# Half of v as seven block products, and the gate row's dot products in quarter pieces: one layer of a gated attention block on one core

## The chip, the cores and the metric

The kernel runs on 1 core of one Trainium2 chip. The metric is device time in microseconds (us) of one execution; lower is better. The core has five engines that work beside each other: TensorE (PE) multiplies matrices, VectorE (DVE) and ScalarE (ACT) work on elements, GpSimd (POOL) here mostly issues adding transfers, and SyncE (SP) issues the plain transfers. Each runs its own list of instructions in order; semaphores tie them together. PE writes its results to PSUM, eight banks of 128 x 512 floats. Everything else lies in SBUF, 128 partitions.

## The reference

One layer, batch 1, 512 tokens, width 2048, float32:

```
shift, scale, gate = silu(c) @ W_ada + b_ada                  # one row each
h = rmsnorm(x) * (1 + scale) + shift
[q_lat|kv_lat|k_rope|z_mla|u|v|z_sgu|g_mla|g_sgu] = h @ W_in
A = causal latent attention(q_lat, kv_lat, k_rope) * silu(z_mla)
B = u * (tril(W_s) @ rmsnorm(v) + b_s) * silu(z_sgu)          # per chunk of 128 tokens, 16 groups
x = x + gate * ((sigmoid(g_mla) * A + sigmoid(g_sgu) * B) @ W_out)
out = rmsnorm(x)
```

What matters here: `v` is 2048 columns of `h @ W_in`, 512 tokens by 2048 inputs. Its groups of 128 columns are needed one by one when B is computed, with a norm over all 2048 columns. The row `gate` is needed only at the very end.

## The kernel before

Each float32 operand of a large product is split in two float32r parts, a high one (a cast on ACT) and the rest (a subtraction on DVE), and each product is three matmuls: high x high, high x low, low x high (`mm3`). Weights come as granules of up to 1024 columns by 128 partitions (512 KB). `Stream` (line 60) loads them into three raw buffers and splits each into one of two pairs of part buffers: `get(i)` (line 110) sees to it that granule i+1 is being split while i is multiplied (`split_to`, line 91) and that loads are issued three ahead (`dma_to`, line 77). A split so waits for PE to finish with the granule two before it.

The work goes in stages, written out by hand:

1. The latent columns, while `scale` and `shift` are made as dot products on DVE: each of 16 rows of W_ada per vector is a transfer of 1 MB (`ada_load`, 306) and one DVE instruction over 2048 elements (`ada_dot`, 312).
2. The v stage (line 511 on): v and the rope key, in five groups of columns, 512, 512, 384, 384 and 320 wide (`VW`, line 38), eight granules each. The tokens' h is stationary, the weights move. A granule holds two of 16 chunks of the inputs; each goes against four blocks of tokens, three matmuls each: 24 matmuls. The groups alternate between two sets of four PSUM banks. After a group, `evac_v` (541) squares and copies one bank per step on ACT and stores it to `v_d` in DRAM. Beside the granules DVE and ACT do the `early` work: latents are scaled and stored (`lat_scale`), sums of h's quarters are made (`make_sums`, 475) and split for the next stage (two of them, s1 and s2, at once; s3 and s4 are kept and split later, s4 in steps 32 to 39, s3 in slots -2 and -1 of the next stage, line 806), and the 16 dot products of `gate` run in steps 8 to 30 (331 to 335), each on a tile of 1 MB loaded through SP's queue.
3. The gate stage: the five gates' 10240 columns as pairs of heads, seven block products per pair (a Strassen-Winograd form: products of sums of h and sums of weights in place of eight products). There it is the weights that are stationary. It has 266 slots, one product each, with an order written by a planner. `on(s, phase, f)` puts a piece of work into slot s; within a slot the lists go FIRST, EVAC, GATE, SPLIT, BACK, then the slot's matmuls, then MISC and LOAD. `place(s, us, f)` (590) seeks the first slot from s on whose DVE time, with the cost `us` given by hand, stays below 2.6 or 2.7 us. The split of a slot's weights is put two slots ahead; there are three pairs of part buffers. Sums of weights are made by transfers that add to what lies in the buffer, issued by POOL.
4. Attention, the output product, the final norm.

Branch B runs inside stage 3, a pair of groups at a time (lines 812 to 857). With S the slot in which the pair's spatial weights are masked: `v_load` (820) fetches each of the two pieces of v, 256 KB, at S-3 into the tiles lat10 (even group) and lat11 (odd); ACT scales the even one in slot S+1 (`sgu_scale`, 828), PE mixes it at the end of S+2 (`sgu_mix`, 833); the odd one is scaled in S+3 and mixed at the end of S+4; DVE adds the bias. There are eight pairs. Such a tile name is one buffer: a new tile of that name waits until the last reader of the old one is done.

Of the kernel before, what the change touches and what calls it, by code (L numbers as in the profile page):

```python
# [37 lines left out]
VW = (512, 512, 384, 384, 320)  # L38
# [21 lines left out]
class Stream:  # L60
# [12 lines left out]
    def add(self, ap, n, to=None):  # L73
        self.src.append((ap, n, to))
        return len(self.src) - 1

    def dma_to(self, i):
        i = min(i, len(self.src) - 1 if self.limit is None else self.limit)
        while self.n_dma <= i:
            k = self.n_dma  # L80
            for f in self.before.pop(k, ()):
                f()
            ap, n, _ = self.src[k]
            pool, tag = self.raws[self.next_raw]
            self.next_raw = (self.next_raw + 1) % len(self.raws)
            t = pool.tile([P, GW], F32, tag=tag, name=f"{tag}_{k}")
            self.nc.sync.dma_start(t[:, :n], ap)
            self.raw[k] = t
            self.n_dma += 1

    def split_to(self, i):
        i = min(i, len(self.src) - 1)
        while self.n_split <= i:
            k = self.n_split
            self.dma_to(k)
            _, n, to = self.src[k]
            raw = self.raw.pop(k)
            self.n_split += 1
            if to is not None:
# [6 lines left out]
            self.nc.scalar.copy(hi[:, :n], raw[:, :n])  # L106
            self.nc.vector.tensor_tensor(out=lo[:, :n], in0=raw[:, :n], in1=hi[:, :n].bitcast(F32), op=ALU.subtract)  # L107
            self.hl[k] = (hi, lo)

    def get(self, i, ahead=1):  # L110
        self.split_to(i + ahead)
        self.dma_to(self.n_split - 1 + len(self.raws))
        return self.hl.pop(i)
# [3 lines left out]
def trunk_layer(ctx, tc, xT, xn, c, vecs, pos, wada, w1, w2, wv, wv3, wv4, wh, wh15, wq, wqr, wk, wvv, wo, wsT, bsp, gfin, out,  # L117
# [77 lines left out]
    dots = nt(cst, [P, 3 * KC], F32, "dots")  # L195
# [13 lines left out]
    gate_row = scratch("gate_row", [KC, P])  # L209
    v_d = scratch("v_d", [NB, P, D])  # L210
# [23 lines left out]
    gv = [ws.add(src[i], 2 * w) for w, src in zip(VW, (wv[0], wv[1], wv3[0], wv3[1], wv4)) for i in range(8)]  # L234
# [96 lines left out]
    gate_step = {}  # L331
    for j in range(KC):
        st = 8 + (3 * j) // 2
        gate_step.setdefault(st, []).append(j)
        load_before(gv[0] + st + 1 if st < 31 else gv[0] + 31, ada_load, 2 * KC + j)
# [126 lines left out]

    def split_sum(name, j, src):
        hilo(sums[name + "h"][:, j], sums[name + "l"][:, j], src)

    def half_of(tags, j):

        if j % 2 == 0:
            halves_[tags, j // 2] = nt(latp.p, [P, S], F32, tags[j // 2])
        return halves_[tags, j // 2][:, (left, right)[j % 2]]  # L470

    halves_, s3f, s4f = {}, {}, {}
    S3_AT, S4_AT = ("lat8", "lat9", "lat12", "lat7"), ("lat0", "lat1", "lat2", "lat3")

    def make_sums(j):
        a, b = (nt(tb.p, [P, S], F32, f"t{i}") for i in range(2))
        tt(a, hh[j].bitcast(F32), hl[j].bitcast(F32), ALU.add)
        tt(b, hh[j + 8].bitcast(F32), hl[j + 8].bitcast(F32), ALU.add)
        s3f[j], s4f[j] = half_of(S3_AT, j), half_of(S4_AT, j)
        tt(s3f[j], a[:, left], a[:, right], ALU.subtract)  # L480
        tt(b[:, right], a[:, right], b[:, right], ALU.subtract)
        tt(a[:, left], b[:, right], a[:, left], ALU.subtract)
        tt(s4f[j], a[:, left], b[:, left], ALU.add)
        return lambda: (split_sum("s1", j, b[:, right]), split_sum("s2", j, a[:, left]))


# [14 lines left out]
    for n, i in enumerate((8, 0, 9, 12, 1, 10, 11, 2, 7, 3, 4, 5, 6)):  # L501
        early.setdefault(8 + n, []).append(lambda i=i: lat_scale(i))

    def sums_begin(j, at_):
        early.setdefault(at_ + 1, []).insert(0, make_sums(j))

    for j in range(8):
        at_ = 12 + 5 * j // 2
        early.setdefault(at_, []).append(lambda j=j, at_=at_: sums_begin(j, at_))
        early.setdefault(32 + j, []).append(lambda j=j: split_sum("s4", j, s4f[j]))  # L510
    for cg, w in enumerate(VW):
        psv = [bank()[:, :w] for _ in range(4)]
        for i in range(8):
            g = cg * 8 + i
            wH, wL = get(gv[g], ahead=1)
            if g < 8:
                fix_to(FIXED[KC + g], lambda: dot_to(DOTS[KC + g]))
            for k in range(2):
                j = 2 * i + k
                sl = slice(k * w, (k + 1) * w)  # L520
                for n in range(NB):
                    tk = slice(n * P, (n + 1) * P)
                    mm3(psv[n], hh[j][:, tk], hl[j][:, tk], wH[:, sl], wL[:, sl], j == 0, j == KC - 1)
            for j in gate_step.get(g, ()):
                ada_dot(2 * KC + j)
            if g == 31:
                ada.close()
                c1[0] = Scope("c1", side=RIGHT)
                sums["s4"] = nt(c1[0].p, [P, 8, 2, 256], F32R, "s4")
                sums["s4h"], sums["s4l"] = sums["s4"][:, :, 0], sums["s4"][:, :, 1]  # L530
            for f in early.pop(g, ()):
                f()
            stores()
        if cg == 0:
            xp.close()
            s12 = Scope("s12")
            for n in ("s1h", "s1l", "s2h", "s2l"):
                sums[n] = nt(s12.p, [P, 8, 256], F32R, n)
            tb = Scope("tB")

        def evac_v(n, cg, ps):
            m = VW[cg] // P
            w, c0 = m * P, sum(VW[:cg])
            junk = nt(tb.p, [P, S], F32, f"t{n % 2}") if cg == 0 else nt(latp.p, [P, S], F32, f"lat{10 + n % 2}")
            ACT.activation(junk[:, :w], ps[:, :w], AF.Square, accum_out=ssv[:, n, cg:cg + 1])
            t = nt(tb.p, [P, S], F32, "sig", bufs=2)
            ACT.copy(t[:, :VW[cg]], ps[:, :VW[cg]])
            store(v_d[n][:, c0:c0 + w], t[:, :w])
            if cg == 4:
                store(kr_d[n], t[:, w:VW[cg]])  # L550

        for n in range(NB):
            pend.append(lambda n=n, cg=cg, ps=psv[n]: evac_v(n, cg, ps))

    def v_norm():
        tt(gate, dots[:, 2 * KC:], vec[:, C_BADA + 2 * KC:C_BADA + 3 * KC], ALU.add)
        DVE.tensor_reduce(out=rv, in_=ssv, axis=AX.X, op=ALU.add)
        rstd_from(rv, rv, D)
# [31 lines left out]
    def place(s, us, f, *a):  # L590

        while busy.get(s, 0.0) + us - 0.07 > (2.6 if 0 <= s < n_slots and order[s][0] in WIDE else 2.7):
            s += 1
        spend(s, us)
        on(s, BACK, f, *a)
        return s
# [208 lines left out]
    for j in range(8):  # L805
        place(-2 + j // 4, 0.42, lambda j=j: hilo(hh[j][:, right], hl[j][:, right], s3f[j]))
# [38 lines left out]
    for p in (7, 0, 1, 2, 3, 4, 5, 6):  # L845
# [30 lines left out]

    on(10, MISC, gate_to_row)
# [257 lines left out]
    def key_rotary(i):  # L1135
        if i == 0:
            kr.extend([slot("lat10"), slot("lat11")])
# [25 lines left out]


# [15 lines left out]

    def sums_of(name):
        return lambda c: (sums[name + "h"][:, c], sums[name + "l"][:, c])

    def quarter(toks):
        return lambda c: (hh[c][:, toks], hl[c][:, toks])

# [503 lines left out]
```

## Time and profile before

| | us |
|---|---|
| median of 3 runs | 1597.05 (1595.55 to 1597.12) |
| the profiled execution | 1596.85 |
| its span, first to last instruction | 1595.1 |
| v stage, first matmul to first matmul after it (154.22 to 337.17) | 182.95 |
| PE busy over the span | 1579.4 |
| DVE busy over the span | 1178.5 |

Rows of a timeline give the start and length in us, the engine, the line of the kernel, the operation, the tile written and the tiles read, partitions x elements, and how many instructions are merged; in brackets the idle time before it and what ended it. Rows of windows give the window, its length, then the busy time and the number of instructions of PE, PEld (weight loads of PE), DVE, ACT and POOL, then the granted PE clock, the mean busy share of the 16 DMA engines, and GB/s. In a row of transfers stand the tiles, the issuing queue, the count, the KB of each, and the median us from issue to landing. A line number can be that of a helper: L136 to L138 are the three matmuls of `mm3`, L106 and L107 the split in `Stream`, L124 and L127 any DVE addition, subtraction or multiply-add. The matmuls of different operands overlap, so their lengths add up to more than the time; from start to start is their true distance.

### The profile page before, as it was taken

To read this page: it belongs to the slowest core of one execution; us is meant where nothing else is said; L and a number is where in the kernel's file an instruction comes from. 1 tells how busy PE (TensorE), PEld (TensorE's weight loads), DVE (VectorE), ACT (ScalarE), POOL (GpSimd) and SP (SyncE) were. 2 spreads that over 40 slices of the span, in tenths; PEclk is the share of its full clock that TensorE was granted. 3 is DMA by queue.
4 is the path that set the end of the run, shared out by engine and by line. 5 is a ranking of instruction groups with operands and counts; after the bars stand their busy time and mean duration, and the time that the engine had idled before them with its cause. 6 is when DMAs were issued, how large, how long until landed. Compare 5 with 4: busy or idle time off the path is not lost.

```text
span 1595.1 us, 25267 instructions
## 1 busy us (share of the span) xinstructions
PE 1579.4 (99%) x9816; PEld 1434.7 (90%) x9816; DVE 1178.5 (74%) x1761; ACT 750.1 (47%) x1291; POOL 104.6 (7%) x128
## 2 busy tenths in 40 slices
PE   9999999999999999999999999999999999999997
PEld 7888889999999999999999999999888889888887
DVE  8989679748787777877777777676777787764453
ACT  4443333456445444454565464554655555542322
POOL 0000000001111111111111011112000000000000
PEclk9999999999999999999999999999999999999999
DMA  9978489569989998888897998977422233336422
GB/s 379 360 288 323 171 284 316 176 189 230 256 237 248 246 255 208 241 241 203 228 257 201 254 268 220 240 194 198 135 87 91 84 105 90 99 118 215 140 84 106
DMA packets 122759, 329.53 MB, mean 207 GB/s; under 512 B 14072, under 2 KB 35600, under 8 KB 115856
## 3 DMA queue, kind: packets, MB, share of 16 engines
q1 hardware_dynamic: 104768, 269.72, 48.4%
q0 software_dynamic: 17872, 58.20, 20.6%
q8 instruction: 77, 1.26, 0.3%
q14 instruction: 42, 0.34, 0.1%
HBM read 303.95 MB, written 23.93 MB: 206 GB/s over the span
## 4 chain that ended last, share of the span: by engine, by line
PE 90%; DVE 4%; DMA 2%; ACT 2%; issue 1%; SPq 0%; DVEq 0%; ACTq 0%
PE ps L136 14%; PE ps L138 14%; PE ps L137 14%; PE ps L1262 12%; PE ps L1270 9%; PE ps L1269 8%; PE ps L1268 8%; PE ps L1264 6%; PE ps L1447 1%; PE ps L837 1%; DVE wada L127 1%; DVE t L124 1%; PE ps L1411 1%; DMA wraw<-in_w 1%; PE ps L1410 1%
## 5 line engine op out<-in xcount | busy, mean ns | idle before, releaser
L124 DVE TENSOR_TENSOR lat<-ps,lat 128x256 f32<-128x256 f32 (+2 forms) x238 | 107.7, 456 | 52.2 <-ACT lat L788 40.1
L107 DVE TENSOR_TENSOR w0l<-wraw,w0h 128x1024 fp32r<-128x1024 f32 (+3 forms) x74 | 79.0, 1068 | 61.8 <-ACT w0h L106 60.9
L106 ACT CAST w0h<-wraw 128x1024 fp32r<-128x1024 f32 (+3 forms) x74 | 69.1, 934 | 107.9 <-PE ps L138 66.7
L106 ACT CAST w1h<-wraw 128x1024 fp32r<-128x1024 f32 (+3 forms) x74 | 63.9, 864 | 118.3 <-PE ps L138 61.0
L107 DVE TENSOR_TENSOR w1l<-wraw,w1h 128x1024 fp32r<-128x1024 f32 (+3 forms) x74 | 73.1, 988 | 61.1 <-ACT w1h L106 60.2
L127 DVE SCALAR_TENSOR_TENSOR wada<-wada,cact 128x2048 f32<-128x2048 f32 x47 | 107.1, 2281 | 0.0
L136 PE MATMUL ps<-w0h,h 128*128 128x256 f32 (+3 forms) x288 | 92.9, 323 | 0.0
L137 PE MATMUL ps<-w0l,h 128*128 128x256 f32 (+3 forms) x288 | 92.6, 321 | 0.0
L138 PE MATMUL ps<-w0h,h 128*128 128x256 f32 (+3 forms) x288 | 92.4, 321 | 0.0
L136 PE MATMUL ps<-h,w1h 128*128 128x512 f32 x226 | 89.9, 398 | 1.0 <-ACT w1h L106 1.0
L137 PE MATMUL ps<-h,w1h 128*128 128x512 f32 x226 | 88.2, 390 | 0.8 <-DVE h L127 0.8
L138 PE MATMUL ps<-h,w1l 128*128 128x512 f32 x226 | 88.3, 391 | 0.0
L634 POOL DMA_DIRECT2D wraw<-in_wh x67 | 59.3, 939 | 434.2 <-DVE w0l L124 175.1
L124 DVE TENSOR_TENSOR w2l<-raw,w2h 128x1024 fp32r<-128x1024 f32 x56 | 68.5, 1223 | 16.0 <-ACT w2h L654 15.6
L136 PE MATMUL ps<-h,w0h 128*128 128x512 f32 x198 | 78.1, 394 | 0.9 <-DVE lat L124 0.9
L138 PE MATMUL ps<-h,w0l 128*128 128x512 f32 x198 | 77.2, 390 | 0.0
L137 PE MATMUL ps<-h,w0h 128*128 128x512 f32 x198 | 77.1, 389 | 0.0
L634 POOL DMA_DIRECT2D raw<-in_wh x42 | 39.6, 980 | 550.4 <-DVE raw L124 338.6
L124 DVE TENSOR_TENSOR w1l<-raw,w1h 128x1024 fp32r<-128x1024 f32 x45 | 55.1, 1224 | 26.1 <-ACT w1h L654 25.9
L654 ACT CAST w2h<-raw 128x1024 fp32r<-128x1024 f32 x56 | 58.9, 1051 | 27.6 <-PE ps L1269 16.5
L124 DVE TENSOR_TENSOR w0l<-raw,w0h 128x1024 fp32r<-128x1024 f32 x46 | 56.3, 1224 | 17.0 <-ACT w0h L654 16.2
L124 DVE TENSOR_TENSOR w0l<-wraw,w0h 128x1024 fp32r<-128x1024 f32 x43 | 52.6, 1223 | 21.5 <-ACT w0h L654 21.2
(349 smaller groups left out, 5139.8 us busy)
## 6 DMA issues: line engine op xcount, KB each, us to landing
raw<-in_wh SPq DMA_DIRECT2D x105, 512.0 KB, 6.9
wada<-in_wada SPq DMA_DIRECT2D x47, 1024.0 KB, 7.6
wraw<-in_wh POOLq DMA_DIRECT2D x67, 512.0 KB, 7.2
wraw<-in_wh SPq DMA_DIRECT2D x45, 512.0 KB, 8.0
raw<-in_wh POOLq DMA_DIRECT2D x42, 512.0 KB, 8.4
wraw<-in_wo SPq DMA_DIRECT2D x32, 512.0 KB, 3.6
half<-in_w SPq DMA_DIRECT2D x35, 256.0 KB, 6.3
wraw<-in_w SPq DMA_DIRECT2D x16, 512.0 KB, 8.4
```

The costliest lines, as they stand in the source:

```text
L106: self.nc.scalar.copy(hi[:, :n], raw[:, :n])
L107: self.nc.vector.tensor_tensor(out=lo[:, :n], in0=raw[:, :n], in1=hi[:, :n].bitcast(F32), op=ALU.subtract)
L124: DVE.tensor_tensor(out=out, in0=in0, in1=in1, op=op)
L127: DVE.scalar_tensor_tensor(out=out, in0=in0, scalar=scalar, in1=in1, op0=op0, op1=op1, **kw)
L136: PE.matmul(ps, ah, bh, start=start, stop=False)
L137: PE.matmul(ps, ah, bl, start=False, stop=False)
L138: PE.matmul(ps, al, bh, start=False, stop=stop)
L634: q_.dma_start(t, wh[h, n, q // 10 - 1], **eng)
L1262: PE.matmul(both, wH[:, cols[c]], xs[c], start=c == 0 and first, stop=False, skip_group_check=True)
L1268: PE.matmul(ps[:, :256], wH[:, cols[c]], xh, start=c == 0 and first, stop=False, skip_group_check=True)
L1269: PE.matmul(ps[:, :256], wH[:, cols[c]], xl, start=False, stop=False, skip_group_check=True)
L1270: PE.matmul(ps[:, :256], wL[:, cols[c]], xh, start=False, stop=c == 7, skip_group_check=True)
```

## The change

**v.** The first 1024 columns of v become block products; the other 1088 (384, 384, 320 wide) stay. The tokens are halved (left, right), the inputs are halved (chunks 0 to 7 and 8 to 15), the columns are halved (two blocks of 512). Seven products p1 to p7 of 256 tokens x 1024 inputs x 512 columns replace eight. The tokens' side is stationary: quarters of h or the sums s1 to s4, which are now all split at once in the v stage. The weights' side are blocks of W and three sums chained in one buffer: loaded for p1, added to for p6, p2 and p4, and one loaded and added to for p3. A product has four granules of two chunks, each chunk against two blocks of tokens: 12 matmuls a granule. The order of the 52 steps:

```
0-7: 384 wide   8-15: 384 wide   16-19: p1   20-23: 320 wide   24-27: p6   28-31: 320 wide
32-35: p2   36-39: p7   40-43: p3   44-47: p5   48-51: p4
```

p1, p2, p3 and p4 accumulate in one pair of banks, p6 and p7 in another, p5 in a third; on the way, copies are kept in SBUF (ACT), and the pieces of v are finished by an addition on DVE and a square on ACT (`quarter_of_v`). The stream gets two more raw buffers and looks nine granules ahead.

**The gate row.** The 16 dot products of 2048 elements leave the v stage; in the gate stage stand 64 of 512 elements, each with a load of 256 KB, alternating between the tiles lat11 and lat12. silu(c) is stored to DRAM and read back in quarters.

**The tiles.** So lat10 alone holds the pieces of v in the gate stage. The split s3 is copied into h's place by transfers.

The core of the diff ("..." marks what is left out):

```diff
-VW = (512, 512, 384, 384, 320)
+VW = (384, 384, 320)
...
+    def adding(src, i, t=None):
+        t = chain[i] if t is None else t
+        nc.gpsimd.dma_start(t, src, accum_op=ALU.add)
+        return t
...
+    for kind, n0, n1 in ((0, 0, 8), (1, 0, 8), ("p1", 0, 4), (2, 0, 4), ("p6", 0, 4), (2, 4, 8), ("p2", 0, 4), ("p7", 0, 4),
+                         ("p3", 0, 4), ("p5", 0, 4), ("p4", 0, 4)):
...
+            elif kind == "p3":
+                g = ws.add(wv[1, i], GW, fetch=lambda t, i=i: adding(wv[1, 4 + i], i, t))
...
-        load_before(gv[0] + st + 1 if st < 31 else gv[0] + 31, ada_load, 2 * KC + j)
+    load_before(g1[3], lambda: DMA.dma_start(c_row, cact[0:1]))
...
+            for hi, lo, src in ((sums["s1h"][:, j], sums["s1l"][:, j], b[:, right]),
+                                (sums["s2h"][:, j], sums["s2l"][:, j], a[:, left]),
+                                (sums["s4"][:, j, 0], sums["s4"][:, j, 1], b[:, left]),
+                                (s3[j][:, 0], s3[j][:, 1], a[:, right])):
+                hilo(hi, lo, src)
...
+    for j, t_ in enumerate((8, 10, 12, 14, 16, 18, 20, 22)):
+        early.setdefault(t_, []).append(lambda j=j, t_=t_: sums_begin(j, t_))
...
+    def quarter_of_v(n, col, ps, junk, what=None, op=None, first=True):
+        if what is None:
+            t = nt(tb.p, [P, S], F32, "sig", bufs=2)
+            ACT.copy(t, ps)
+        else:
+            t = kept_v.pop((what, n % 2))
+            if first:
+                tt(t, ps, t, op)
+            else:
+                tt(t, t, ps, op)
...
+        ACT.activation(junk, t, AF.Square, accum_out=ssv[:, n, 3 + col:4 + col])
+        store(v_d[n][:, col * S:(col + 1) * S], t)
...
+    for t_, (kind, i) in enumerate(steps):
...
+        wH, wL = get(gv[t_])
...
+            ws.more_raws([(c1[0].p, "w2h"), (c1[0].p, "w2l")])
+            ws.look = 9
...
+                for n in range(2):
+                    tk = slice(n * P, (n + 1) * P)
+                    ps = psv[b_][n]
+                    st = c == 0 and kind in ("p1", "p6", "p5")
+                    for m, (x_, w_) in enumerate(((xh, wH), (xh, wL), (xl, wH))):
+                        PE.matmul(ps, x_[:, tk], w_[:, sl], start=st and m == 0, stop=c == 7 and m == 2, skip_group_check=True)
...
     for j in range(8):
-        place(-2 + j // 4, 0.42, lambda j=j: hilo(hh[j][:, right], hl[j][:, right], s3f[j]))
+        on(-2 + j // 4, LOAD, lambda j=j: DMA.dma_start(hx[j][:, :, right].bitcast(F32), s3[j].bitcast(F32)))
...
     def v_load(g):
-        sgw["v", g % 2] = v = nt(latp.p, [P, NB, P], F32, f"lat{10 + g % 2}")
+        sgw["v", g % 2] = v = nt(latp.p, [P, NB, P], F32, "lat10")
...
-        for q in range(2):
-            on(s_ - 3, LOAD, v_load, 2 * p + q)
+        on(s_ - 3, LOAD, v_load, 2 * p)
         s_ = place(s_, 0.42, sgu_weights)
         for q in range(2):
             g = 2 * p + q
             on(s_ + 1, BACK, sgu_scale, q)
             s_ += 2
             on(s_, MISC, sgu_mix, q)
+            if q == 0:
+                on(s_, LOAD, v_load, g + 1)
...
+    def gate_dot(q, j, n):
+        t = gp.pop(n)
+        stt(t, t, 1.0, gp["c"], ALU.mult, ALU.mult, accum_out=dots[:, q % 2 * KC + j:q % 2 * KC + j + 1])
...
+    used = [sgu_end[7] + 2] * 2
+    for n in range(4 * KC):
+        q, j = divmod(n, KC)
+        free = used[-1] if j == 0 else used[-2]
+        on(free, LOAD, gate_load, q, j, n)
+        used.append(place(max(free + 4, used[-1] + 1), 0.8, gate_dot, q, j, n, room=0.15))
+    on(used[-1] + 1, MISC, gate_to_row)
```

More of the change, by code (lines that the diff above doesn't have):

```diff
@@ L461, in trunk_layer @@
     left, right = slice(0, S // 2), slice(S // 2, S)
[L463 to L473, printed above, removed]
+    S3_AT = ("cosT", "sinT", "lat8", "lat9", "lat12", "lat1", "lat7", "lat10")
+    s3 = []
     def make_sums(j):
@@ L499, in lat_scale @@
         store(lat_d[i], lat[i])
[L501 to L517, printed above, removed]
+    for t_, i in zip((2, 3, 4, 5, 6, 7, 8, 14, 16, 20, 22, 29, 31), (8, 9, 12, 1, 7, 10, 11, 0, 2, 3, 4, 5, 6)):
+        early.setdefault(t_, []).append(lambda i=i: lat_scale(i))
@@ L533, in trunk_layer @@
[L533 to L550, printed above, removed]
@@ L555, in v_norm @@
+        for f in early.pop(t_, ()):
+            f()
+        stores()
+    assert not early
+    ws.raws, ws.look = [(wp, f"wraw{i}") for i in range(3)], 3
     def v_norm():
-        tt(gate, dots[:, 2 * KC:], vec[:, C_BADA + 2 * KC:C_BADA + 3 * KC], ALU.add)
         DVE.tensor_reduce(out=rv, in_=ssv, axis=AX.X, op=ALU.add)
@@ L588, in spend, with place @@
         busy[s] = busy.get(s, 0.0) + max(us - 0.07, 0.0)
-    def place(s, us, f, *a):
-        while busy.get(s, 0.0) + us - 0.07 > (2.6 if 0 <= s < n_slots and order[s][0] in WIDE else 2.7):
+    def place(s, us, f, *a, room=0.0):
+        while busy.get(s, 0.0) + us - 0.07 > room + (2.6 if 0 <= s < n_slots and order[s][0] in WIDE else 2.7):
             s += 1
@@ L1136, in key_rotary @@
         if i == 0:
-            kr.extend([slot("lat10"), slot("lat11")])
+            kr.extend([slot("lat10"), half_raw(1)])
             swapped(kr[3], kr[0])
```

160 lines of the change are left out of this document (123 added, 37 removed).

## The prediction

> **What bounds the kernel now.** I read the page's first and fourth parts, then windows over the stage that computes v and over the stage of the gates, then the timelines of TensorE (PE), VectorE (DVE) and ScalarE (ACT) inside them.
>
> ```profile
> PE 1579.4 (99%) x9816; PEld 1434.7 (90%) x9816; DVE 1178.5 (74%) x1761; ACT 750.1 (47%) x1291; POOL 104.6 (7%) x128
> PE 90%; DVE 4%; DMA 2%; ACT 2%; issue 1%; SPq 0%; DVEq 0%; ACTq 0%
> ```
>
> The matmuls are the chain. A busy PE isn't yet a PE at its peak, so I took the distance from start to start, in the v stage.
>
> ```profile
> 154.22:337.17 182.95, 182.75 (x961) 166.66 (x960) 132.65 (x185) 68.38 (x125) 0.00 (x0) 1.00 0.70 240
> ```
> ```profile
> 184.82 0.39 PE L136 MATMUL ps<-w1h,h 128*128 128x512 f32 x1
> ...
> 229.25 0.39 PE L137 MATMUL ps<-w1l,h 128*128 128x512 f32 x1
> ```
> ```profile
> 284.45 0.33 PE L138 MATMUL ps<-w0h,h 128*128 128x384 f32 x1
> ...
> 293.29 0.33 PE L138 MATMUL ps<-w0h,h 128*128 128x384 f32 x1
> ```
> ```profile
> 336.73 0.31 PE L136 MATMUL ps<-w1h,h 128*128 128x320 f32 x1
> ...
> 337.17 0.39 PE L136 MATMUL ps<-h,w0h 128*128 128x512 f32 x1
> ```
>
> 196 steps lie between the first two rows: 0.2267 us for a matmul of 512 columns. 51 lie between the next two: 0.1733 for 384. Three lie between the last two: 0.147 for 320. The stage has 384 + 384 + 192 of them, 87.1 + 66.6 + 28.2 = 181.8 us, of its 182.95 us (the first number after the window, above). So 1.1 us of it is waiting, and whatever takes a matmul away there shortens the kernel, as long as nothing else becomes late.
>
> **The matmuls removed.** Two 512-column groups are 16 granules x 24 = 384 matmuls. Seven products are 28 granules x 12 = 336, of the same shape. 48 fewer x 0.2267 = **-10.9 us**, and it is all on the path. The Trainium skill (TensorE: Matmul & The Clock Gate, section on the 56 ns gap) puts a warm matmul at N / 2.4 GHz + 2.5 ns, 215.7 ns here; as an estimate by that page the term would be -10.4. The trace's pitch decides.
>
> **The old waits.** The v stage's 1.1 us of waits stand among the 2.28 us dot products of the gate row, which leave: **-1.1 us** (bounds 0 and -1.1).
>
> **What is late next: the split.** A granule of 512 columns lasted 5.44 us; a product's granule lasts 12 x 0.2267 = 2.72. There are two buffers, so granule t+1 is split while t runs. ACT and DVE run their lists in order.
>
> ```profile
> 197.74 0.39 PE L136 MATMUL ps<-w0h,h 128*128 128x512 f32 x1
> ```
> ```profile
> 197.94 1.05 ACT L106 CAST w1h<-wraw 128x1024 fp32r<-128x1024 f32 x1 [4.34 <-PE ps L138]
> 198.90 0.59 ACT L545 ACTIVATE t<-ps 128x512 f32<-128x512 f32 x1
> ...
> 199.47 0.58 ACT L547 COPY sig<-ps 128x512 f32<-128x512 f32 x1
> ```
> ```profile
> 199.03 1.23 DVE L107 TENSOR_TENSOR w1l<-wraw,w1h 128x1024 fp32r<-128x1024 f32 x1 [4.17 <-ACT w1h L106]
> 200.17 2.28 DVE L127 SCALAR_TENSOR_TENSOR wada<-wada,cact 128x2048 f32<-128x2048 f32 x1
> 202.38 0.69 DVE L124 TENSOR_TENSOR lat<-lat,rx 128x512 f32<-128x512 f32 x1
> ```
>
> From a granule's first matmul at 197.74 the cast starts 0.20 later, DVE's part starts at 1.29 and ends at 2.52. The second matmul of the next granule, which needs it, is due at 2.72 + 0.23 = 2.95. The slack is 0.4 us. Three things lie in its way.
>
> (a) Evacuations with an add (products 7, 3 and 5, two each, in consecutive steps). The add is queued on DVE behind the split (free at 2.43) and ends at 3.12; the square on ACT waits for it and frees ACT near 3.73 (0.57 from its start at 198.90 to the next at 199.47); the next cast would have begun at 2.92. It is 0.8 late: 0.4 of waiting for the first, and 0.8 for the second, which inherits the first's delay. Behind the waiting square stand ACT's next cast, DVE's next split and PE. 3 x 1.2 = **+3.7 us** (bounds 0 and 5).
>
> (b) The sums of step 16 and 18, beside product 1.
>
> ```profile
> 224.75 1.28 DVE L124 TENSOR_TENSOR t<-h 128x512 f32<-128x512 f32 x2
> ...
> 227.54 1.22 DVE L107 TENSOR_TENSOR w0l<-wraw,w0h 128x1024 fp32r<-128x1024 f32 x1
> 228.67 0.42 DVE L124 TENSOR_TENSOR s1l<-t,s1h 128x256 fp32r<-128x256 f32 x1
> 229.01 0.42 DVE L124 TENSOR_TENSOR s2l<-t,s2h 128x256 fp32r<-128x256 f32 x1
> ```
>
> A sum takes DVE 2.79 us (224.75 to 227.54) and its splitting 0.34 a quarter, now four instead of two: 1.36. Steps 16 to 19 ask 2 x (2.79 + 1.36) + 3 x 1.14 + 0.8 (the 320-column split) + 0.6 (a latent scaled) = 13.1 us of DVE in 10.9 us of PE: **+2.0 us** (0 to 3.5). The other sums stand beside granules of 4.16 and 3.53 us and fit.
>
> (c) The first group is now 384 columns wide, so the last shifts have 33 us and not 43. By the same lists DVE is behind once, near step 6: **+0.4** (0 to 1.1).
>
> Product 3's weights are loaded and then added to by a transfer, five steps ahead.
>
> ```profile
> wraw<-in_wv SPq DMA_DIRECT2D x16, 512.0 KB, 4.1
> ```
> ```profile
> wraw<-in_wh POOLq DMA_DIRECT2D x67, 512.0 KB, 7.2
> ```
>
> 4.1 + 7.2 and an issue are 11.5 to 12 us; five steps less the wait for the buffer are 13.6 - 2.3 = 11.3: **+0.5** (0 to 2). The other added weights have eight steps.
>
> **Between the stages.** Eight splits on ACT and DVE in slots -2 and -1 become eight SBUF copies on SP's queue.
>
> ```profile
> PE ps L1262 <- ACT lat L774: 0.8, 1, 0.8
> ```
>
> This wait, at the gates' start, is behind them: **-0.8** (0 to -0.8). The copies read what was split long before; the weights and the first v piece queued behind them on SP are needed ten microseconds later.
>
> **The gate row's pieces.** 64 dot products, by this row 0.75 us each:
>
> ```profile
> 415.30 0.75 DVE L127 SCALAR_TENSOR_TENSOR rx<-cosT,shift,rx 128x512 f32<-128x512 f32 x1
> ```
> ```profile
> 350.00:770.00 420.00, 419.19 (x3049) 398.10 (x3048) 329.22 (x453) 206.50 (x307) 52.29 (x61) 1.00 0.89 234
> ```
>
> Following the planner's own costs, the first falls in slot 15 and the last in slot 258 of 266, and a slot's DVE work never passes 2.9 us, with one slot in hand, so DVE hides them. Their 16.8 MB over some 700 us are 24 GB/s; the stage moves 234 GB/s at a DMA share of 0.89, so the share becomes 0.98. 64 issues join SP's queue, each waiting for a dot product of the same slot. **+0.5** (0 to 12).
>
> **The v pieces in the gates.** Here is the price that I think decides. lat11 and lat12 went to the gate row, so both groups of a pair use lat10: the odd group's piece can't be requested until PE has finished the even group's mix, and the next slot's ACT list scales it.
>
> ```profile
> 800.41 1.06 PE L837 MATMUL ps<-wsr,lat 128*128 128x128 f32 x8
> ...
> 806.89 1.06 PE L837 MATMUL ps<-wsr,lat 128*128 128x128 f32 x8
> ```
> ```profile
> 801.44 1.28 ACT L831 ACTIVATE lat<-lat,rv 128x128 f32<-128x128 f32 x4
> ```
>
> The even mix ends at 801.47, ACT scales the odd piece at 801.44, the odd mix runs at 806.89. So 5.4 us now hold the load and the 1.28 us of scaling: 4.1 for the load. PE keeps its order, so a late load stops it at the odd mix; on ACT the casts and evacuations of two slots are queued behind the scaling, and on SP the later loads behind the request. Landing times of this load, first for the four of the first two pairs, then for the twelve others:
>
> ```profile
> DMA to landing us min/median/max: 3.2/3.9/4.9
> ```
> ```profile
> DMA to landing us min/median/max: 6.7/8.0/9.7
> ```
> ```profile
> half<-in_w SPq DMA_DIRECT2D x35, 256.0 KB, 6.3
> ```
> ```profile
> 598.30:603.70 5.40, 5.40 (x33) 4.72 (x32) 3.50 (x4) 2.84 (x7) 0.82 (x1) 1.00 0.68 232
> 699.60:705.00 5.40, 5.40 (x33) 4.72 (x32) 2.06 (x3) 2.84 (x7) 0.00 (x0) 1.00 1.01 341
> ```
>
> The twelve were requested in twos; a lone load of that size takes 6.3. The two windows run from an even mix to its odd one; the last number but one is the DMA share. It is 1.01 in the second, and 0.68 in the mildest of the eight: the load would join a full queue. I take 7.0: 7.0 - 4.1 = 2.9 us, six times, and 1 us for each of the first two pairs: **+19.4 us** (0 at 3.2 us, 45 at 9.7).
>
> **The sum.** -10.9 - 1.1 + 3.7 + 2.0 + 0.4 + 0.5 - 0.8 + 0.5 + 19.4 = +13.7. The profiled execution took 1596.85 us (span 1595.1), 0.2 below the median of the three runs, so the forecast is 1610.5 us.
>
> **Rivals.** *Fast loads* (faster). The same sum with the v piece landing inside 4.1 us is -5.7: 1591.2 us. That limit is the point from which it decides. For it: 3.2 to 4.9 in the first two pairs, the window at 0.68, and that a waiting PE lets the DMA engines empty. Against: not one of the later twelve was under 6.7. The Trainium skill (DMA: Bandwidth & Descriptors, anatomy of the SWDGE path) fits a transfer as 2.0 us plus its bytes over 436 GB/s. By it 256 KB land in 2.6 us, an estimate by which this rival would hold; the trace disagrees, with 3.2 as its shortest. *Full DMA.* The gate pieces lift the share from 0.89 to 1, and every odd piece takes 9.7: 8 x 5.6 = 45 in place of 19.4, 1636 us. For it: windows at 1.0 already; against: the mean stays below. The skill's TensorE page (HAM oscillation) adds that an idle PE of some 3.4 us halves its clock; no trace here shows it. *Split-bound products.* The slack of 0.4 us is lost in all 28 granules, by a late raw load or a slower list: 28 x 0.4 = 11 us more, 1621 us; without v waits 1602.
>
> **How the numbers follow.** Forecast 0.70, fast loads 0.15, full DMA 0.08, split-bound 0.07. The forecast's own range, with loads of 5.9 to 8.2 us, is 1602 to 1620. To leave out no more than two in ten, the range reaches down to the fast loads' 1591 and up past the split-bound case to 1625. 0.2% (3.2 us) is about what a measurement of this kernel can tell from no change. Slower: nearly all of the forecast and both slow rivals, less the short-load edge, 0.78; within 0.2%: 0.06; faster: 0.16.
>
> **What would show it.** Right: from the even to the odd mix 8 us and more instead of 6.48 from start to start, ACT's scaling (L831's line) waiting on the load of v, eight waits of PE at the odd mixes; the v stage near 171 + 6.6 = 177.5 us, with PE waits in steps 16 to 20 and 42 to 50. Wrong: odd mixes at the old distance, or loads of v landing in under 4.1 us; a v stage of 183 or more; DVE waiting for gate pieces.

## The result and the profile after

The changed kernel takes 1624.66 us (median of 4 runs, 1623.67 to 1625.66), the kernel before beside it 1596.78: a ratio of 1.0176, 95% interval 1.0158 to 1.0194. It is slower, as forecast, but by 27.9 us and not by 13.7. The profiled execution took 1625.66 us with a span of 1624.0, so the spans differ by 28.8.

From the page of the kernel after, the busy time and the chain:

```profile
PE 1578.4 (97%) x9768; PEld 1424.3 (88%) x9768; DVE 1199.2 (74%) x1878; ACT 763.3 (47%) x1303; POOL 118.4 (7%) x144
PE 84%; DMA 7%; DVE 5%; ACT 2%; issue 1%; SPq 0%; DVEq 0%; ACTq 0%
```

PE's part of the chain fell from 90% to 84%, that of transfers rose from 2% to 7%. Windows over the v stage and the gate stage after, and the gate stage before (columns as told above):

```profile
155.57:342.69 187.12, 179.42 (x914) 159.97 (x912) 119.67 (x179) 85.06 (x151) 13.82 (x16) 0.98 0.68 188
342.69:1154.96 812.27, 788.03 (x5672) 742.43 (x5670) 633.40 (x922) 401.87 (x590) 102.41 (x117) 0.99 0.90 247
```
```profile
337.17:1124.90 787.73, 785.90 (x5672) 744.05 (x5671) 600.34 (x799) 405.41 (x604) 102.38 (x117) 1.00 0.86 229
```

The v stage has 48 matmuls less and is 4.2 us longer (187.12 against 182.95; I had 177.5). The gate stage is 24.5 us longer. Both show a granted clock below 1.00, which the kernel before nowhere does while it multiplies. What PE waited for, after (rows of waits give who waited for whom, the us in total, how often, and the longest):

```profile
PE ps L931 <- ACT lat L925: 20.2, 8, 4.8
PE ps L633 <- DVE w0l L118: 2.2, 2, 1.4
PE ps L147 <- ACT w0h L117: 1.9, 1, 1.9
```

The first row is the odd mix of B: eight waits, 20.2 us, the shortest 0.2 and the longest 4.8. One of them in the timelines of PE, ACT and SP:

```profile
507.36 1.06 PE L931 MATMUL ps<-wsr,lat 128*128 128x128 f32 x8
516.32 2.07 PE L931 MATMUL ps<-wsr,lat 128*128 128x128 f32 x8 [2.34 <-ACT lat L925]
```
```profile
508.45 0.38 SPq L916 DMA_DIRECT2D lat<-v_d  x1
```
```profile
515.87 1.28 ACT L925 ACTIVATE lat<-lat,rv 128x128 f32<-128x128 f32 x4 [7.38 <-DMA lat<-v_d]
```

The piece of v is requested when the even mix has ended, ACT stands 7.4 us until it has landed, and the odd mix starts 8.96 us after the even one, in place of 6.48. In seven of the eight pairs the distance is 8.9 to 11.4 us, in one 6.8.

And the clock, in windows around a longer wait:

```profile
928.97:932.38 3.41, 0.00 (x0) 0.00 (x0) 0.75 (x1) 0.00 (x0) 0.00 (x0) 1.00 1.00 374
932.38:939.20 6.82, 5.57 (x18) 4.80 (x19) 3.26 (x6) 4.34 (x9) 0.84 (x1) 0.50 0.58 173
```

PE is idle for the first window; in the second the last column but two, the granted clock, is 0.50, and matmuls of 512 columns stand 427 ns apart. Such a stretch at a granted clock of 0.5 is called half clock here.

To see what made the difference I took, for each stage, the distance from each matmul to the next, and counted what lies above the usual distance of its shape as waiting, or as half clock where the granted clock was 0.5. What is left is the pitch, the distance between matmuls that do not wait. Changes against the kernel before, in us:

| stage | forecast | measured | of it waits | half clock | pitch | matmuls removed |
|---|---|---|---|---|---|---|
| up to v | 0 | +1.3 | +0.1 | 0 | +1.2 | |
| v | -5.4 | +4.2 | +10.1 | +3.0 | +2.0 | -10.9 |
| gates | +19.1 | +24.5 | +25.8 | +9.3 | -10.7 | |
| the rest | 0 | -1.2 | -0.5 | 0 | -0.7 | |

Three things stand in it that the sum did not have: half clock (12.3 us), a wait in the v stage that I had not seen, and a pitch that changed under work that the change does not touch.

The wait is in steps 11 and 12 of the v stage. Timelines of ACT and SP:

```profile
206.33 0.48 ACT L552 COPY sig<-ps 128x384 f32<-128x384 f32 x1 [7.51 <-DMA v_d<-sig]
```
```profile
196.34 2.08 SPq L250 DMA_DIRECT2D raw<-in_wv  x4
198.46 0.43 SPq L529 DMA_DIRECT2D v_d<-sig  x1
```

An evacuation copies into one of two buffers; the third copy waits for the store of the first. With the stream now looking nine granules ahead, four loads of 512 KB for product 1 were issued just ahead of that store. ACT stood 7.5 us, and behind its copy the next cast: PE lost 2.9 us, with half clock behind it.

### The profile page after: what moved, and what is told of

The parts are those of the page before. It is cut to its first block, busy times and chain, and to the rows that moved or that the text cites. A ratio compares the mean times of both kernels' runs of the same rounds, so it can differ in the third digit from the quotient of the medians.

```text
span 1624.0 us, 25494 instructions
## 1 busy us (share of the span) xinstructions
PE 1578.4 (97%) x9768; PEld 1424.3 (88%) x9768; DVE 1199.2 (74%) x1878; ACT 763.3 (47%) x1303; POOL 118.4 (7%) x144
## 4 chain that ended last, share of the span: by engine, by line
PE 84%; DMA 7%; DVE 5%; ACT 2%; issue 1%; SPq 0%; DVEq 0%; ACTq 0%
PE ps L149 13%; PE ps L148 13%; PE ps L147 13%; PE ps L1371 10%; PE ps L1379 8%; PE ps L1377 8%; PE ps L1378 8%; PE ps L1373 5%; DMA lat<-v_d 4%; PE ps L633 3%; PE ps L1556 1%; PE ps L931 1%; PE ps L1520 1%; DMA b<-latn_d 1%; DMA wraw<-in_w 1%
## 5 line engine op out<-in xcount | busy, mean ns | idle before, releaser
L135 DVE TENSOR_TENSOR lat<-ps,lat 128x256 f32<-128x256 f32 (+3 forms) x242 | 110.4, 459 | 35.5 <-ACT lat L882 23.4
L118 DVE TENSOR_TENSOR w0l<-wraw,w0h 128x1024 fp32r<-128x1024 f32 (+2 forms) x67 | 71.6, 1068 | 49.1 <-ACT w0h L117 48.5
L118 DVE TENSOR_TENSOR w1l<-wraw,w1h 128x1024 fp32r<-128x1024 f32 (+3 forms) x66 | 64.4, 976 | 56.3 <-ACT w1h L117 55.4
L117 ACT CAST w0h<-wraw 128x1024 fp32r<-128x1024 f32 (+2 forms) x67 | 62.5, 934 | 82.7 <-PE ps L149 32.1
L117 ACT CAST w1h<-wraw 128x1024 fp32r<-128x1024 f32 (+3 forms) x66 | 56.3, 854 | 92.5 <-PE ps L149 31.6
L138 DVE SCALAR_TENSOR_TENSOR wada<-wada,cact 128x2048 f32<-128x2048 f32 x31 | 70.6, 2278 | 0.0
L147 PE MATMUL ps<-w0h,h 128*128 128x256 f32 (+2 forms) x224 | 68.0, 303 | 1.9 <-ACT w0h L117 1.9
L148 PE MATMUL ps<-w0l,h 128*128 128x256 f32 (+2 forms) x224 | 67.7, 302 | 1.0 <-DVE w0l L118 1.0
L149 PE MATMUL ps<-w0h,h 128*128 128x256 f32 (+2 forms) x224 | 67.3, 300 | 0.0
L748 ACT CAST w1h<-raw 128x1024 fp32r<-128x1024 f32 x45 | 47.2, 1049 | 42.5 <-DVE raw L135 29.0
```

Of the source, the lines that this page charges most:

```text
L135: DVE.tensor_tensor(out=out, in0=in0, in1=in1, op=op)
L147: PE.matmul(ps, ah, bh, start=start, stop=False)
L148: PE.matmul(ps, ah, bl, start=False, stop=False)
L149: PE.matmul(ps, al, bh, start=False, stop=stop)
L748: ACT.copy(hi, src)
```

## Experiments: the gate stage

**Theory.** The late piece of v stops PE, as forecast, and a wait that is long enough costs a second time: the next 3.4 us run at half clock. Rivals: the late piece stands for full DMA engines, so something else is late once it is not; or the matmuls are slow for another reason than idleness.

**The odd group two slots later**, for six of eight pairs:

```diff
-            on(s_ + 1, BACK, sgu_scale, q)
-            s_ += 2
+            s_ += 2 + (2 * q if p not in (7, 0) else 0)
+            on(s_ - 1, BACK, sgu_scale, q)
```

> Changed kernel, with the odd group's scaling and mix two slots later for six of the eight pairs (all but the first two in time), so that the piece of v has about 10 us to land in place of 4.1; no tile is added. My theory: the odd mixes wait for the piece of v (20.2 us in all in the changed kernel's trace, about 16 of it at these six), and each wait long enough also brings a stretch of 3.4 us at half the granted clock (five such stretches in the gate stage, 9.2 us of slow matmuls, 7.5 of it at these six). Both go: 1624.7 - 16 - 7.5 = 1601 us, no wait of PE at these six mixes, and one stretch at half clock left in the gate stage. Rival (the late piece stands for a full DMA, so that other loads come late in its place): the waits move to the splits, 1615 us or more. Rival (the slow matmuls come from something else): 1608 us, half clock still there.

1605.59 us (1603.81 to 1609.88), ratio to the kernel before 1.0059 (1.0042 to 1.0076). Its waits of PE at the mixes:

```profile
PE ps L931 <- ACT lat L925: 5.7, 2, 3.0
```

Only the two pairs that were left alone still wait. The gate stage is 19.4 us shorter than in the changed kernel, 15.0 of it waits and 4.3 half clock. The waits did not move to the splits, so the first rival falls. The median is 4.6 us above my figure. The trace is of the slowest of the four executions (1609.88): there three half-clock stretches stand in the gates where I expected one, and the v stage, which this edit does not touch, is 2.9 us longer than in the changed kernel, by waits and half clock. How much of that the other three executions had is not known.

**The kernel before with that one sharing:**

```diff
-        sgw["v", g % 2] = v = nt(latp.p, [P, NB, P], F32, f"lat{10 + g % 2}")
+        sgw["v", g % 2] = v = nt(latp.p, [P, NB, P], F32, "lat10")
...
-        for q in range(2):
-            on(s_ - 3, LOAD, v_load, 2 * p + q)
+        on(s_ - 3, LOAD, v_load, 2 * p)
...
             on(s_, MISC, sgu_mix, q)
+            if q == 0:
+                on(s_, LOAD, v_load, g + 1)
```

> Kernel before, with one edit: both pieces of v of a pair share one tile, so the odd one is loaded after the even mix. The gate row stays in the v stage, v is not a block product. My theory: this alone brings the waits at the odd mixes and the half clock behind them: 15 to 20 us of waits and 5 to 9 us of slow matmuls, 1597 + 25 = 1622 us (1616 to 1627). Rival (the gate row's 64 loads fill the DMA engines, and only with them is the piece late): under 5 us of waits, no half clock, 1602 us or less.

1616.31 us (1614.41 to 1617.60), ratio 1.0123 (1.0106 to 1.0139). Waits and a window behind the longest:

```profile
PE ps L837 <- ACT lat L831: 11.0, 7, 3.8
```
```profile
923.70:930.53 6.83, 6.23 (x21) 5.46 (x22) 3.92 (x5) 4.58 (x9) 0.84 (x1) 0.50 0.66 207
```

One shared tile, with no gate pieces and no block products, costs 19.3 us: 14.5 of waits in the gate stage (11.0 at the mixes) and 4.8 of half clock. The waits are shorter than with the gate pieces (11.0 against 20.2), so the sharing makes the wait, and something else in the changed kernel lengthens it. Four odd pieces that both traces follow to their landing took 6.4, 5.8, 4.0 and 6.4 us here, and 7.7, 7.3, 5.2 and 7.4 in the changed kernel. The first odd piece, which the changed kernel requests before its first gate load, took 8.6 us here and 7.6 there. So the 64 gate loads are the likely cause, but they were not tried alone. The total stays 6 us below the 1622 that I expected.

**Filling the wait** with 2.0 us of matmuls that add nothing to the output:

```diff
+        for _ in range(17 * q):
+            PE.matmul(flat[:, :S // 2], hh[0][:, :P], hh[1][:, left], start=True, stop=True)
```

> Changed kernel, with 17 matmuls of 256 columns (2.0 us) put ahead of each odd mix, into the bank that the mix then overwrites; they add nothing to the output. My theory: the half clock follows from idle time of PE (on a grid of 3.41 us, stretches with over about 2 us idle are followed by a slow one, those with under 1.8 are not), so with 2.0 us of each wait filled four or five of the five slow stretches in the gate stage go: -7 to -9, and +2 where the wait was shorter than the filling: 1618.5 us (1617 to 1621). Rival (the slow matmuls come from what arrives late together with the wait, splits or transfers): the slow stretches stay, and the filling costs 2: 1626.5 us.

1622.48 us (1621.42 to 1625.98), ratio 1.0165 (1.0149 to 1.0180). The same stretch of the gate stage with and without filling:

```profile
341.45:1130.00 788.55, 778.52 (x5687) 735.72 (x5686) 617.53 (x900) 389.23 (x571) 102.42 (x117) 1.00 0.91 249
```
```profile
342.69:1130.00 787.31, 765.00 (x5509) 720.92 (x5508) 613.86 (x892) 386.23 (x567) 101.57 (x116) 0.99 0.91 249
```

All five half-clock stretches at the mixes are gone, though the pieces are as late as before (five odd ones landed in 5.6 to 7.8 us, the same five in 5.2 to 7.7 without filling): they follow from PE's idle time. The gain was smaller than I wrote (2.2 us): the filling took 16 us and the waits shrank by only 10.7, and one new half-clock stretch stood at the stage's end.

## Experiments: the v stage

**A shorter look ahead** until step 12 (`ws.look = 5`, then 9):

> Changed kernel, with the stream of the v stage looking five granules ahead until step 12 and nine from there on, so that the four loads of 512 KB for product 1 are not issued just ahead of the first store of v. My theory: in steps 11 and 12 ACT stood 7.5 us at its third evacuation until that store had left its buffer, PE waited 2.9 us behind it, and 1.4 us of slow matmuls followed; both go, and nothing else is late, as product 1 is needed from step 16 on: 1624.7 - 4.3 = 1620.4 us. Rival (the store is slow whatever stands ahead of it, or product 1 then comes late): 1623.5 us or more.

1621.43 us (1620.79 to 1623.28), ratio 1.0156 (1.0141 to 1.0171). The v stage:

```profile
155.92:337.96 182.04, 175.90 (x913) 157.49 (x912) 119.65 (x179) 85.19 (x151) 13.82 (x16) 1.00 0.70 193
```

187.12 became 182.04: the wait at steps 11 and 12 is gone, and so is all half clock of this stage. The next three were built on this kernel and are read by their v stage, since the number of half-clock stretches in the gates differed from build to build (7.6 us here, 12.1, 9.9 and 12.4 in the next three).

**Product 3 without the adding transfer**, its second block left out:

```diff
-                g = ws.add(wv[1, i], GW, fetch=lambda t, i=i: adding(wv[1, 4 + i], i, t))
+                g = ws.add(wv[1, i], GW)
```

> The kernel with the shorter look ahead (1621.4 us; its waits of PE in the v stage: 9.2 us, 4.2 of them in steps 40 to 43, 2.4 in steps 18 to 20, 1.1 in 46 and 47, 1.15 in 50 and 51), with product 3's weights loaded only: the transfer that adds the second block is left out, so product 3 is computed from one block. My theory: the waits of steps 40 to 43 are mostly product 3's added weights (8.1 us to land, on top of the load), and 1.1 is product 7's evacuation: -3.1, 1618.3 us. Rival (the evacuation with its add is the whole of it): the 4.2 stay, 1621 us.

1621.88 us (1619.04 to 1623.36), ratio 1.0154 (1.0139 to 1.0169). Waits of PE from 296 to 318 us, first with the transfer, then without:

```profile
PE ps L635 <- DVE w1l L118: 1.2, 2, 0.8
PE ps L635 <- ACT w1h L117: 1.1, 1, 1.1
PE ps L635 <- DVE w0l L118: 0.8, 1, 0.8
```
```profile
PE ps L635 <- DVE w1l L118: 0.5, 1, 0.5
```

By distances, steps 40 to 43 wait 1.15 us in place of 4.2, so 3.0 us were the added weights and 1.15 product 7's evacuation. The v stage lost only 1.8 us, as 1.5 appeared at steps 35 and 36, and the time as a whole did not fall (my 1618.3 was wrong): the gates had more half clock. So the cause rests on these waits and not on the time.

**Squares two steps after their adds:**

```diff
-        ACT.activation(junk, t, AF.Square, accum_out=ssv[:, n, 3 + col:4 + col])
-        store(v_d[n][:, col * S:(col + 1) * S], t)
+        def finish():
+            ACT.activation(junk, t, AF.Square, accum_out=ssv[:, n, 3 + col:4 + col])
+            store(v_d[n][:, col * S:(col + 1) * S], t)
...
+            pend.append(finish)
```

> The kernel with the shorter look ahead (1621.4 us), with the squares of the pieces of v from products 7, 3 and 5, and their stores, done two steps after their adds, so that ACT's list never waits for DVE's add. My theory (term a of the prediction): the waits of steps 46, 47, 50 and 51 go, 2.3 us, and some 1 us of those in steps 40 to 43: -2.3 to -3.4, 1618.5 us. Rival (the add itself, behind the split on DVE, is what is late): no change, 1621 us.

1619.84 us (1619.71 to 1621.07), ratio 1.0146 (1.0129 to 1.0163). The waits of steps 46 to 51, 2.3 us with the square behind the add, of which this row is a part,

```profile
PE ps L635 <- DVE w1l L118: 1.0, 2, 0.5
```

are zero now. Steps 40 to 43 wait 4.8, so the 1 us that I hoped for there did not come; product 3's weights come when they come.

**Sums earlier**, begun in steps 8, 9, 10, 12, 13, 14, 20 and 22:

> The kernel with the shorter look ahead (1621.4 us), with the eight sums begun in steps 8, 9, 10, 12, 13, 14, 20 and 22 instead of every second step from 8 to 22, so that none stands beside product 1 (steps 16 to 19). My theory (term b of the prediction): the 2.4 us of waits in steps 18 to 20 go, and the second group's granules of 4.16 us hold six sums: 1619.0 us. Rival (DVE is then late in steps 9 to 15): the wait moves there, 1621 us or more.

1626.96 us (1620.96 to 1629.25), ratio 1.0182 (1.0162 to 1.0203). The 2.4 us of steps 18 to 20 went, but 1.5 came in steps 11 and 12, 0.9 in 15 and 16, and 2.9 with half clock behind it in 20 and 21. ACT's row says what the last is:

```profile
ACT sig L552 <- DMA v_d<-sig: 8.3, 3, 5.6
```

It is again a copy that waits for a store. Term (b) was there, and moving it was no gain by the medians; the trace is of the slowest execution (1629.25), and the fastest took 1620.96.

**All together**, with the odd group two slots later for seven pairs and lat11 for the first pair's odd piece (the gate pieces take lat11 only later):

> All of it together: shorter look ahead, squares later, sums earlier, and for the odd pieces of v: the first pair's has lat11, which the gate row's pieces take up only later, and the other seven pairs' are scaled and mixed two slots later. My theory: of the changed kernel's 20.2 us of waits at the odd mixes and 9.3 us of half clock in the gate stage nearly all go (some 27), in the v stage 5 go beside the 5.1 that the shorter look gave: 1624.7 - 5 - 27 - 5 = 1588 us (1585 to 1592), below the kernel before. Rival (a full DMA moves the waits elsewhere in the gates): 1595 us or more.

1591.89 us (1587.40 to 1598.95), ratio 0.9970 (0.9958 to 0.9982). The gate stage's waits are 9.4 us and its half clock 1.6, so that part held. The trace is of the slowest of ten executions (1598.95), and in it the v stage took 187.1:

```profile
242.81 0.48 ACT L552 COPY sig<-ps 128x384 f32<-128x384 f32 x1 [7.93 <-DMA v_d<-sig]
```

**Without the earlier sums, and with the second two evacuations of the first two plain groups, and one of the third's, in free latent tiles:**

```diff
+        tag = {(0, 2): "lat1", (0, 3): "lat7", (1, 2): "lat10", (1, 3): "lat11", (2, 2): "lat11"}.get((cg, n))
+        t = nt(latp.p, [P, S], F32, tag) if tag else nt(tb.p, [P, S], F32, "sig", bufs=2)
```

> The kernel with everything together, but the sums begun in steps 8 to 22 as in the changed kernel, and the second two evacuations of each of the three plain groups of v into free latent tiles (lat1, lat7, lat10, lat11), so that no evacuation waits for the store of the one two before it. My theory: the 5.0 us wait and 2.7 us of half clock at steps 20 and 21 go, which were this same wait for a store (ACT stood 7.9 us), and steps 18 to 20 wait 2.4 again: v stage 180 us, the whole 1589 us (1586 to 1592). Rival (the late store has moved only because of the sums): no change against 1591.9.

1590.28 us (1587.48 to 1594.79), ratio 0.9961 (0.9948 to 0.9974): no wait for a store is left, the v stage takes 179.85, with 4.5 us of waiting and half clock left in steps 41 to 43. The median differs from the kernel's above by 1.6 us, less than the spread of either, so it is the trace and not the time that shows this.

**And a sixth raw buffer from step 24 on**, the two tiles of the sums as one:

```diff
+        if t_ == 24:
+            ws.more_raws([(tb.p, "t01")])
...
```

> The same with one more raw buffer for the stream from step 24 on (the two tiles of the sums as one of 512 KB, free by then), so that product 3's weights are loaded one granule earlier. My theory: the 4 to 5 us of waits in steps 40 to 43, which come from its load and the adding transfer behind it (3 us of them went when the adding transfer was left out), shrink by 2 to 4 us: 1586 us. Rival (the adding transfers wait for something else than their buffers): 1589 us.

1585.34 us (1583.60 to 1587.49), ratio 0.9931 (0.9916 to 0.9945). Its two stages:

```profile
155.54:330.87 175.33, 173.45 (x913) 157.72 (x912) 119.70 (x179) 84.96 (x151) 13.82 (x16) 1.00 0.73 202
```
```profile
330.87:1115.59 784.72, 778.30 (x5671) 734.92 (x5670) 632.79 (x922) 401.56 (x587) 102.22 (x117) 1.00 0.93 256
```

No wait is left in steps 40 to 43. At equal places of the tiles the mended change so stands 4.8 us under the kernel before (1590.1, below); the two ranges do not meet.

One more wait stands in these traces. At the gate stage's end PE waits for an addition on DVE, first in the kernel before, then in the changed one, then here:

```profile
PE ps L1262 <- DVE lat L124: 0.9, 1, 0.9
PE ps L1371 <- DVE lat L135: 1.9, 1, 1.9
PE ps L1386 <- DVE lat L135: 2.5, 1, 2.5
```

In the last one half clock stands behind it. The last gate piece's product, its sum and the row's copy stand on DVE in the 7 us ahead of that addition. The kernel before with the shared tile alone waits 0.9 as well, so the wait grew with the rest of the change; that it is the gate pieces was not tried alone.

## Experiments: the pitch

The change also makes the small tile `dots` 64 bytes per partition narrower, so the tiles allocated behind it on that side (the part buffers and the sums among them) lie 64 bytes lower. **The changed kernel with the old width, nothing else:**

```diff
-    dots = nt(cst, [P, 2 * KC], F32, "dots")
+    dots = nt(cst, [P, 3 * KC], F32, "dots")
```

> Changed kernel with one edit: the tile dots is again 48 columns wide, as in the kernel before, of which 16 are not used. That moves every tile behind it by 64 bytes per partition, to where the kernel before has them. No wait is touched. My theory: the pitch of the matmuls depends on where their operands lie: those of 256 columns in the gates go from 117.5 back to 119.8 ns (+10.4 us), those of 512 in the first stages from 228.6 to 226.6 and in the products from 231.5 to 226.7 (-1.3 and -1.6), the rest of the kernel +1.2: 1633 us (1629 to 1637). Rival (the pitch follows the order of the work or the transfers beside it): 117.5 stays, 1624.7 us.

1634.67 us (1632.40 to 1636.79), ratio 1.0239 (1.0223 to 1.0254). The same 24 matmuls of the same slot, first and twenty-fifth start, in the changed kernel and in this one:

```profile
437.38 0.28 PE L1377 MATMUL ps<-s2h,w2h 128*128 128x256 f32 x1
...
440.11 0.28 PE L1377 MATMUL ps<-h,w1h 128*128 128x256 f32 x1
```
```profile
437.39 0.28 PE L1377 MATMUL ps<-s2h,w2h 128*128 128x256 f32 x1
...
440.27 0.28 PE L1377 MATMUL ps<-h,w1h 128*128 128x256 f32 x1
```

2.73 us there, 2.88 here: 114 and 120 ns a matmul.

**The kernel before with the new width** (the gate row's sums in the scale row's columns):

> Kernel before with one edit: the tile dots is 32 columns wide instead of 48 (the gate row's sums take the columns that the scale row no longer needs), which moves every tile behind it by 64 bytes per partition, as in the changed kernel. My theory: 119.8 becomes about 117.5 ns for the 256-column matmuls of the gates (-10.4 us), 226.6 becomes 228.6 for those of 512 in the first two stages (+1.2 and +0.8), the rest -1.2: 1597 - 9.6 = 1587.5 us (1585 to 1592). Rival (the pitch is the change's, not the place's): 1597 us.

1590.14 us (1589.42 to 1590.89), ratio 0.9959 (0.9945 to 0.9974). Gate stages of the two, to be read against the two gate windows shown first:

```profile
341.63:1163.21 821.58, 797.30 (x5671) 752.02 (x5670) 634.51 (x922) 401.83 (x590) 102.42 (x117) 0.99 0.89 244
```
```profile
341.09:1118.92 777.83, 775.19 (x5673) 733.13 (x5672) 599.13 (x799) 405.63 (x604) 102.34 (x117) 1.00 0.87 232
```

Mean pitch in ns, of matmuls that did not wait:

| kernel | 512 columns, up to v | 512, v stage | 256, gates | us |
|---|---|---|---|---|
| before | 226.6 | 226.7 | 119.8 | 1596.8 |
| before, 64 bytes lower | 228.6 | 233.3 | 117.4 | 1590.1 |
| after | 228.6 | 231.5 | 117.5 | 1624.7 |
| after, at the old place | 226.5 | 227.8 | 119.8 | 1634.7 |

The pitch goes with the place, both ways. (In the gates the matmuls of 512 columns keep theirs: 229.6 ns before, 229.4 after.) By place alone a kernel gains some 6 to 10 us; at equal places the change as made costs 34.5 us (1624.7 - 1590.1) or 37.9 (1634.7 - 1596.8), not 27.9.

## Why the prediction was right in direction and short in size

The mechanism was the one that I named: the odd pieces of v stop PE, for 20.2 us where I had 19.4. The size was short by half. The step that failed is the last term, "The v pieces in the gates": **+19.4 us** priced the waits alone, and 9.3 us of half clock stood behind them. The v stage, which I had 5.4 us shorter, became 4.2 longer; a v stage of 183 us or more was one of my own signs of being wrong, and it came.

That the range, 1591 to 1625, holds 1624.66 is luck. The tiles' new place, which the sum did not have, hid some 10 us: at the old place the changed kernel takes 1634.7.

- *The matmuls removed, -10.9.* The count holds. The pitch that I multiplied with holds at the old place only (227.8 ns there): 231.5 ns for the products after, +1.6 us.
- *The old waits, -1.1.* Gone.
- *(a) evacuations with an add, +3.7.* Right: 1.15 us for each of the three (steps 46 and 47, steps 50 and 51, and product 7's, the last as read without product 3's adding transfer), 3.5 in all. The first two went with the squares later.
- *(b) sums beside product 1, +2.0.* 2.4 measured; the working, 13.1 less 10.9, gives 2.2. *(c), +0.4:* 0.3.
- *Product 3's weights, +0.5.* Too small: 3.0 in the kernel with the shorter look ahead. The load took 5.0 us and the adding transfer 8.1 (medians after), where I had 4.1 and 7.2 from the kernel before: 13.1 against the 11.3 that five steps leave.
- *Missing:* the store of v behind the four loads for product 1, 2.9 us. I had followed the looking ahead for what is needed, not for what is queued behind it.
- *Between the stages, -0.8.* Of the wait 0.5 is left.
- *The gate pieces, +0.5.* DVE hides them, except perhaps at the stage's end, where PE waits 1.0 us more than before, and the gate stage's DMA share is 0.90 (0.86 before), not 0.98. What they cost was not tried alone; in the last kernel, which has them, the gate stage waits 8.9 us against 5.7 before. Beside the shared tile they may cost more: 20.2 against 11.0.
- *The v pieces, +19.4.* Waits at the odd mixes: 20.2. Behind them came 9.3 us of half clock. I had a rule of that kind in hand and set it aside because "no trace here shows it". A trace without long waits cannot show it: the forecast itself made six waits of 2.9 us and two of 1, and that is where such a rule should have been priced. As I had it, with a limit of some 3.4 us, it would have charged none of them; the limit that the runs show is about 2 us (last section). The other 5.6 us of waiting stand in small pieces behind the mixes and, 1.0 us of it, at the stage's end; I did not take them apart.

So the terms were 12.3 us short for the clock and 11 for waits, and the pitch gave 8 back over the whole span. Of the rivals, fast loads fell: the six odd pieces that the trace follows landed in 5.2 to 9.8 us. Full DMA held only in part: the stage's mean share stayed at 0.90, but while the odd pieces were under way it was 0.96 to 1.05; they took 7.5 us in the middle and not 9.7, and one of the eight made PE wait only 0.2 us. Split-bound products did not come, as waits stood in at most 11 of the products' 28 granules and not in all.

## What to carry to other kernels

A wait of PE of two microseconds or more can cost its length and then some 1.6 us again: behind five of the seven waits of that length at the changed kernel's mixes a half-clock stretch followed. So price both, and where a wait can't be avoided, split it or give PE work. A tile freed for one purpose is a prefetch taken from another: ask how long the load now has, and what stands in its queue. Before a few microseconds are put down to a change, see whether matmuls that it did not touch kept their pitch.

## What the runs showed of the hardware

**Half clock after about 2 us of idleness.** The stretches of half clock last 3.413 us or twice that (but for the one behind each run's last matmuls), and their starts in a run lie multiples of 3.413 us apart, so they sit on a fixed grid. I added up PE's idle time in each cell of that grid, from 100 us to the last matmuls, for the changed kernel and the eleven experiments that showed such stretches. All 50 half-clock stretches start behind cells with 2.01 us or more of idle time, and no cell with more than 2.07 us went without. The idle time need not be in one piece: at 307.7 us of the changed kernel several short waits made 2.3. A wait of that length that lies across a border of two cells can go free, as those at 380.5 and 721.9 us did (2.5 and 2.4 us). A stretch of 3.4 us cost some 1.4 to 1.8 us. Within half clock another limit shows, with idle time counted against twice the usual distance: the 11 slow cells with 0.9 us or more of it were followed by a second slow one, and the 50 with 0.7 or less were not. The Trainium skill (TensorE: Matmul & The Clock Gate, HAM oscillation) puts the limit at idle gaps of more than some 3.4 us, and its first part says that the window is 3413 ns long and free-running. The window agrees; the limit here was lower, 2.0 to 2.1 us within it, so waits between 2 and 3.4 us, which that rule passes, were charged where they fell into one cell.

**The place of a tile changes the pitch of matmuls**: 64 bytes per partition moved the 256-column matmuls of the gates by 2.3 ns of 119.8 on average, and those of 512 columns in the first two stages by 2 to 7 ns the other way. At the old place nearly all of the 256-column ones stand 120 ns apart; at the new one it goes by the tiles they read, for instance 114 ns for h against w1h, 118 against w0h and 120 against w2h, each followed by its like. Which addresses go well together was not tried.
